# Wide norm factors: the row statistic by a ones-stationary matmul and one Newton step on a [128x256] tile in SBUF

## The chip, the core and the metric

The kernel runs on one core of one Trainium2 chip. The metric is the device time of one execution in microseconds (us), lower is better. A core has five engines that run their own instruction queues in order: TensorE (PE in the profile, with its weight loads as PEld), VectorE (DVE), ScalarE (ACT), GpSimd (POOL) and SyncE (SP, which only issues DMAs). They wait for each other on semaphores. PE writes into PSUM, here eight banks of [128x512] float32; the other data lie in SBUF.

## What is computed

A trunk of two layers on x of 512 tokens by 1024 channels, in float32. Layer 0 mixes tokens with stick-breaking attention, layer 1 with a diagonal state-space layer; each is followed by a gated MLP with a short causal convolution. Ahead of each of these four sub-layers, and once more at the end, stands an RMS norm, modulated by a conditioning vector:

```python
def rms_norm(x, g):
    y = x * lax.rsqrt(jnp.mean(x * x, axis=-1, keepdims=True) + EPS)
    return y * g

for i in range(DEPTH):                      # DEPTH = 2
    h = modulate(rms_norm(x, norm_mix[i]), sh1, sc1)
    x = x + g1 * (attention(h) if i == 0 else s5_ssm(h))
    h = modulate(rms_norm(x, norm_ffn[i]), sh2, sc2)
    x = x + g2 * conv_ffn(h)
return modulate(rms_norm(x, norm_out), sh, sc)
```

This case is about the factor rsqrt(mean(x*x) + EPS), one number per token, of which there are five sets of 512.

## The kernel before, in words

**Layout.** x lies in SBUF as eight tiles x[k] of [128 channels x 512 tokens] (`KD` = 8). The sum over channels is therefore a sum over the eight tiles and over the 128 partitions. Each product of the big matrices is made as three matmuls of a high and a low part (`mm3`, L169 to L175: L171 high by high, L174 high weights by low activations, L175 low weights by high activations), each 128x512, or 128x256 where only half of the tokens is done. `HALF` is the pair of token halves, columns 0 to 255 and 256 to 511.

**A joint.** Between two sub-layers the kernel does not wait for the norm of all tokens. `out_proj` (L360) makes the last product of a sub-layer: output tiles mt by mt, each added to x[mt] by `resid` (L350, DVE, L355), whose square (ACT, L244) is added to the running sum `acc` (DVE, L245). The last `TAIL` = 3 tiles (4 before the end of the program) are done for the first token half and then for the second (L404 to L416). While PE does the second half, the norm of the first half is worked out, and `head_mm` (L326) starts the next sub-layer's first four products with the first half, then does the second half, and the channels k = 6 and 7 for both. There are four joints: attention to MLP 0, MLP 0 to state-space layer, state-space layer to MLP 1, MLP 1 to output.

**The factor before.** For one half of a joint `rstd_stat` (L278) calls `rstd_y` (L258): for each 128 tokens a matmul with those columns of `acc` as stationary operand and a single column of ones as moving operand, which leaves the sums with tokens on partitions, a [128x2] tile in the PSUM bank `stat` (L266). ACT takes the square root (`nsd`, L270), DVE makes v (L271), the reciprocal (L272) and one Newton step of the inverse root (L273 to L275) on [128x2]. Two DVE instructions scale the unit matrix by it into `dg` (L283), a [128x256] tile of two diagonal blocks. Then `rstd_bc` (L286) multiplies ones with `dg` (L288): each of the 128 partitions of the PSUM bank `rbc` now holds the factor of each token along the free dimension, as `norm_tile` (L302) needs it for x * factor (DVE, L308). ACT then applies the modulation twice, to `hH` (L315) and to `nt` (L317), and DVE makes the low part `hL` (L321).

**What sets the order.** A scheduler orders each engine's queue, except for instructions that are pinned to their written order (`pe_pin`). The matmuls of the factor are pinned at a chosen place of PE's queue: the first half's `stat` ahead of product k = `STATK` = 0 of the second-but-last tile of the tail, and its `rbc` at `MIDK` or `MIDN` of the next tile; the second half's at `HEADS` = (1, 2) and `HEADB` = (3, 2) in the head, which are (k, product). So the factor's way through ACT and DVE is covered by matmuls that stand between.

**The two other uses.** At the program's start `rstd_y` is called for all 512 tokens (L605), and the start has `dg` and `rbc` of its own (L609 to L618). At the end, `last` (L1503) norms the first half as channels by tokens (`ft`, L1527 on DVE for k = 0, L1529 on POOL for the others, from an SBUF copy `bcs` of `rbc`, L1506; then ACT, L1531) and the second half as tokens by channels: `xa` (L1511, POOL) is transposed by PE, and the factor `y` of `rstd_y` (L1520, with `sq` of the last tile, L1508, as a second part) is a scalar per partition in L1543 (ACT, then POOL L1544) and L1546 (DVE). Eight stores follow (L1535, L1547).

Of the kernel before, what the change touches and what calls it, by code (L numbers as in the profile page):

```python
# [7 lines left out]
F32 = mybir.dt.float32  # L8
# [3 lines left out]
AF = mybir.ActivationFunctionType  # L12
ALU = mybir.AluOpType
# [3 lines left out]
P = 128  # L17
T = 512
D = 1024
# [9 lines left out]
NC = T // CH  # L29
EPS = 1e-6  # L30
NW = 5
MIDK = 1
STATK = 0
HEADK = 6
HEADS = (1, 2)
HEADB = (3, 2)
HEADW = (4, 8, 11, 13)
UPRE = 12
NACC = 6
# [20 lines left out]
NPRE = 3  # L60
KPRE = 5
NWT = 4
MIDN = 2
TAIL = 3
QK = 'kq'
BGA = 3
# [23 lines left out]
def _trunk(ctx, tc, I, out, tap):  # L90
# [10 lines left out]
    np_ = pool("np")  # L101
# [4 lines left out]
    def bank(p=None, name="ps"):  # L106
        p = p or mm
        return p.tile([P, 512], F32, tag="b", name=name)
# [14 lines left out]
    ident = consts[:, 0:128]  # L123
# [121 lines left out]
            V.tensor_tensor(acc[:, cr], acc[:, cr], sq[:, cr], ALU.add)  # L245

    def rstd_new(acc):
        return dict(acc=acc, ps=bank(aux, "stat"), dg=np_.tile([P, T], F32, tag="dg", bufs=1, name="dg"), bc={})

    def pe_pin(ins):  # L250
        tc.keep_in_program_order(ins)
# [1 line left out]
    def sqrt_table():  # L253

        warm = np_.tile([P, 64], F32, tag="warm", bufs=1, name="warm")[:, 0:1]
        tc.keep_in_program_order(S.activation(warm, ones[:, 0:1], AF.Sqrt))

    def rstd_y(R, cr, pinned=False, more=(), between=lambda: None):  # L258
        t0, t1 = cr.start // P, cr.stop // P
        ps = R["ps"]  # L260
        parts = [R["acc"]] + list(more)
        for q, part in enumerate(parts):
            if q:
                between()
            for i in range(t0, t1):
                ins = PE.matmul(ps[:, i:i + 1], part[:, i * P:(i + 1) * P], ones[:, 0:1], start=q == 0 and (i == t0 or len(parts) == 1), stop=q == len(parts) - 1 and (i == t1 - 1 or q == 0))  # L266
                if pinned:
                    pe_pin(ins)
        v, sd, y, t = (np_.tile([P, 4], F32, tag=g, bufs=2, name=g)[:, :t1 - t0] for g in ("nv", "nsd", "ny", "ntm"))
        R["nsd"] = S.activation(sd, ps[:, t0:t1], AF.Sqrt, bias=epst, scale=1.0 / D)  # L270
        V.tensor_scalar(v, ps[:, t0:t1], 1.0 / D, EPS, ALU.mult, ALU.add)  # L271
        V.reciprocal(y, sd)  # L272
        V.tensor_tensor(t, y, y, ALU.mult)  # L273
        V.scalar_tensor_tensor(t, v, -0.5, t, ALU.mult, ALU.mult)
        V.scalar_tensor_tensor(y, t, 1.5, y, ALU.add, ALU.mult)  # L275
        return y

    def rstd_stat(R, cr, pinned=False):  # L278
        t0, t1 = cr.start // P, cr.stop // P
        dg = R["dg"]  # L280
        y = rstd_y(R, cr, pinned)
        for i in range(t0, t1):
            ins = V.tensor_scalar(dg[:, i * P:(i + 1) * P], ident, y[:, i - t0:i - t0 + 1], None, ALU.mult)  # L283
        return ins

    def rstd_bc(R, cr, pl, pinned=False):  # L286
        bc = bank(pl, "rbc")
        ins = PE.matmul(bc[:, cr], ones, R["dg"][:, cr], start=True, stop=True)  # L288
        if pinned:
            pe_pin(ins)  # L290
        R["bc"][cr.start] = bc

    def new_h():
        hh = [hp_.tile([P, T], F32R, tag=f"hH{k}", name=f"hH{k}") for k in range(KD)]
# [31 lines left out]
    def head_mm(R, h, a, b, hd):  # L326
        pin["head"] = []
        todo = [(k, HALF[0]) for k in range(HEADK)] + [(k, HALF[1]) for k in range(HEADK)] + [(k, FULL) for k in range(HEADK, KD)]
        made = 0
        for n, (k, cr) in enumerate(todo):  # L330

            while made < (min(n + 3, HEADK) if cr == HALF[0] else n + 1):
                norm_tile(h, todo[made][0], R["bc"], a, b, todo[made][1])
                made += 1
            for q, (w, ps) in enumerate(hd):
                if cr == HALF[0] and (k, q) == HEADS:
                    rstd_stat(R, HALF[1], True)
                if cr == HALF[0] and (k, q) == HEADB:
                    rstd_bc(R, HALF[1], mm, True)
                mm3(ps[:, cr], wk(w, k), (h[0][k][:, cr], h[1][k][:, cr]), k == 0 and cr.start == 0, k == KD - 1)  # L340

    @contextmanager
# [17 lines left out]
    def out_proj(wsrc, rhs, gcol, acc2, nm, tail=TAIL, perm=False, n=D, after=lambda: None, part=(), last=None, head=None, getw=None, step=lambda: None, early={}):  # L360
# [46 lines left out]
        for q, (mt, w, ps) in enumerate(ws):  # L407
            mid = {}
            if q == 1:
                mid[STATK] = lambda: rstd_stat(R, ca, True)  # L410
            if q == 2:
                mid[MIDK if nk > 6 else MIDN] = lambda: rstd_bc(R, ca, aux, True)
            run(ps, w, cb, mid, pinned=True)
            if last and mt == KD - 1:
                resid(mt, ps, gate(mt), cb, None, perm)
                last(R)  # L416
            else:
                resid(mt, ps, gate(mt), cb, acc2, perm)
# [1069 lines left out]
    with ExitStack() as fctx:  # L1488
# [13 lines left out]

        def last(R):  # L1503
            op, a, brow = F_["op"], F_["a"], F_["brow"]
            bcs = op.tile([P, H], F32, tag="bcs", name="bcs")
            bci = S.activation(bcs, R["bc"][0][:, ca], AF.Copy)  # L1506
            sq = op.tile([P, T], F32, tag="sq", name="sq7")
            sqi = V.tensor_tensor(sq[:, cb], x[KD - 1][:, cb], x[KD - 1][:, cb], ALU.mult)  # L1508
            xa = [op.tile([P, H], F32, tag=f"xa{k}", name=f"xa{k}") for k in range(KD)]
# [13 lines left out]
            for q, k in enumerate(FORD):  # L1523
                t = op.tile([P, H], F32, tag="t", bufs=4, name="ft")
                with behind_head([sqi] if k else [bci]), behind_head([R["nsd"]]) if q >= FINA else ExitStack():
                    if k < FINV:
                        V.tensor_tensor(t, x[k][:, ca], R["bc"][0][:, ca], ALU.mult)  # L1527
                    else:
                        G.tensor_tensor(t, x[k][:, ca], bcs, ALU.mult)  # L1529
                    if q < FINS:  # L1530
# [108 lines left out]
```

## Time and profile before

| | |
|---|---|
| runs (3) | median 1175.27 us, 1175.04 to 1179.25 us |
| the profiled execution: span from the first to the last instruction | 1174.0 us (the profile gives no other time of its own for that execution) |
| granted TensorE clock, mean | 0.995 |
| PE busy | 1158.9 us, 99% of the span, 6242 matmul records |
| DVE, ACT, POOL busy | 857.7 us (73%), 563.5 us (48%), 270.8 us (23%) |
| DMA | 211.01 MB, mean 180 GB/s |

How to read it. Times are in us from the start of the span, unless marked ns. A row of the timeline gives start, duration, engine, line of the kernel, operation, output<-inputs with shapes, how many instructions are merged, and in brackets how long the engine was idle before it and what ended that. The chain of waits is followed back from the last instruction; its rows give start, duration, engine, tile and line. A float32 matmul (`stat`, `rbc`) leaves two records each. Matmul records overlap, so the cost of a matmul on PE is read from the starts of its neighbours or from the chain, not from its duration.

### The profile page before, as it was taken

What the parts mean: (1) busy time and instruction counts of PE and PEld (TensorE: products, weight loads), DVE (VectorE), ACT (ScalarE), POOL (GpSimd) and SP (SyncE); (2) the same over time, 40 slices, a digit from 0 to 9 for tenths busy, and PEclk for the clock granted to TensorE, in tenths of its full rate; (3) what the DMA queues carried; (4) which work ended last, traced back from release to release, by engine and by line L of the source; (5) the groups of instructions that cost most, each with busy time, mean ns of one, the idle gap of its engine ahead of it and who ended that gap; (6) DMA issues with size and microseconds to landing.
All of it is one profiled execution on the core that took longest, in us unless ns stands there. A gap on an engine that the chain in (4) does not pass through costs nothing.

```text
span 1174.0 us, 16592 instructions
## 1 busy us (share of the span) xinstructions
PE 1158.9 (99%) x6242; PEld 964.2 (82%) x6242; DVE 857.7 (73%) x1311; ACT 563.5 (48%) x896; POOL 270.8 (23%) x278
## 2 busy tenths in 40 slices
PE   8999999999999999999999999999999999999997
PEld 7887777699788888888889888789888888888887
DVE  6968888775998666787757599887598378744555
ACT  6756667456453244413346477647443144422443
POOL 2001110000298799979800000000000000000003
PEclk8999999999999999999999999999999999999999
DMA  8873656331267858797756598671176357432322
GB/s 320 292 264 116 192 162 195 111 123 55 78 189 268 247 167 252 198 292 253 230 151 223 149 353 293 207 255 50 49 231 217 107 153 184 133 123 73 92 69 72
DMA packets 91618, 211.01 MB, mean 180 GB/s; under 512 B 19601, under 2 KB 37905, under 8 KB 91538
## 3 DMA queue, kind: packets, MB, share of 16 engines
q1 hardware_dynamic: 78562, 191.08, 51.0%
q0 software_dynamic: 4656, 16.78, 4.5%
q10 hardware_dynamic: 8320, 2.10, 0.8%
q8 instruction: 49, 0.80, 0.3%
q14 instruction: 31, 0.25, 0.1%
HBM read 188.68 MB, written 21.24 MB: 179 GB/s over the span
## 4 chain that ended last, share of the span: by engine, by line
PE 78%; DVE 7%; issue 7%; DMA 5%; ACT 2%; POOL 1%; SPq 1%; POOLq 0%; DVEq 0%; ACTq 0%
PE up L171 13%; PE up L174 13%; PE up L175 13%; PE dn L171 6%; PE dn L174 6%; PE dn L175 6%; DMA wg<-in_w_modT_dram 3%; PE u L174 1%; PE u L171 1%; PE u L175 1%; PE wo L171 1%; PE wos L174 1%; PE wo L175 1%; PE wo L174 1%; PE wos L175 1%
## 5 line engine op out<-in xcount | busy, mean ns | idle before, releaser
L171 PE MATMUL up<-hH,up_h 128*128 128x512 f32 x640 | 249.7, 391 | 0.3 <-DVE ca L461 0.3
L175 PE MATMUL up<-hH,up_l 128*128 128x512 f32 x640 | 249.3, 390 | 0.3 <-DVE up_l L166 0.3
L174 PE MATMUL up<-hL,up_h 128*128 128x512 f32 x640 | 249.3, 390 | 0.0
L461 DVE SCALAR_TENSOR_TENSOR ca<-up,small,ca 128x511 f32<-128x511 f32 (+1 forms) x176 | 131.6, 748 | 120.7 <-ACT ca L459 117.6
L171 PE MATMUL dn<-gH,dn_h 128*128 128x512 f32 (+1 forms) x394 | 145.0, 369 | 0.0
L198 DVE SCALAR_TENSOR_TENSOR wg<-wg,cact 128x1024 f32<-128x1024 f32 x96 | 121.4, 1281 | 31.7 <-DMA wg<-in_w_modT_dram 31.6
L174 PE MATMUL dn<-gL,dn_h 128*128 128x512 f32 (+1 forms) x394 | 144.5, 367 | 0.0
L175 PE MATMUL dn<-gH,dn_l 128*128 128x512 f32 (+1 forms) x394 | 144.4, 366 | 0.0
L171 PEld LDWEIGHTS up<-hH,up_h 128*128 128x128 f32 x640 | 120.1, 188 | 26.5 <-issue 1.5
L175 PEld LDWEIGHTS up<-hH,up_l 128*128 128x128 f32 x640 | 120.1, 188 | 25.9 <-DVE up_l L166 1.1
L174 PEld LDWEIGHTS up<-hL,up_h 128*128 128x128 f32 x640 | 120.1, 188 | 24.4
L459 ACT ACTIVATE ca<-up,small 128x512 f32<-128x512 f32 x88 | 68.2, 775 | 149.5 <-PE up L175 149.5
L1511 POOL TENSOR_SCALAR xa<-x,Anorm_out 128x256 f32<-128x256 f32 x7 | 5.7, 818 | 570.3 <-DVE x L355 570.3
L165 ACT ACTIVATE up_h<-up_r 128x1024 fp32r<-128x1024 f32 x80 | 84.2, 1052 | 75.3 <-PE dn L174 58.1
L166 DVE TENSOR_TENSOR up_l<-up_r,up_h 128x1024 fp32r<-128x1024 f32 x80 | 116.3, 1454 | 5.4 <-ACT up_h L165 4.5
L355 DVE SCALAR_TENSOR_TENSOR x<-dn,mod,x 128x512 f32<-128x512 f32 (+1 forms) x55 | 37.4, 680 | 71.4 <-PE dn L175 71.4
L171 PEld LDWEIGHTS dn<-gH,dn_h 128*128 128x128 f32 x394 | 74.3, 189 | 12.9 <-issue 0.6
L174 PEld LDWEIGHTS dn<-gL,dn_h 128*128 128x128 f32 x394 | 74.3, 189 | 12.1
L175 PEld LDWEIGHTS dn<-gH,dn_l 128*128 128x128 f32 x394 | 74.3, 189 | 12.1
L165 ACT ACTIVATE dn_h<-dn_r 128x1024 fp32r<-128x1024 f32 (+1 forms) x48 | 46.7, 982 | 46.2 <-PE dn L174 38.5
L166 DVE TENSOR_TENSOR dn_l<-dn_r,dn_h 128x1024 fp32r<-128x1024 f32 (+1 forms) x48 | 61.6, 1283 | 0.8 <-ACT dn_h L165 0.5
L477 ACT ACTIVATE gH<-gm 128x512 fp32r<-128x512 f32 x44 | 27.1, 616 | 67.3 <-DVE gm L473 67.3
(349 smaller groups left out, 2311.0 us busy)
## 6 DMA issues: line engine op xcount, KB each, us to landing
up_r<-in_w_up_dram SPq DMA_DIRECT2D x80, 512.0 KB
wg<-in_w_modT_dram SPq DMA_DIRECT2D x71, 512.0 KB
dn_r<-in_w_down_dram SPq DMA_DIRECT2D x32, 512.0 KB
wg<-in_w_modT_dram POOLq DMA_DIRECT2D x25, 512.0 KB, 4.0
wgs<-in_w_modT_dram SPq DMA_DIRECT2D x16, 512.0 KB
dn_r<-in_w_down_dram SPq DMA_DIRECT2D x16, 384.0 KB
wv_r<-in_w_v_dram SPq DMA_DIRECT2D x8, 512.0 KB
wk_r<-in_w_qk_dram SPq DMA_DIRECT2D x8, 512.0 KB
```

The source lines that it names most:

```text
L165: order("S", lambda: S.activation(wh[:, :n], raw[:, :n], AF.Copy))
L166: pin["split"] = order("V", lambda: V.tensor_tensor(wl[:, :n], raw[:, :n], wh[:, :n].bitcast(F32), ALU.subtract))
L171: ins = PE.matmul(ps, ah, bh, start=start, stop=False)
L174: PE.matmul(ps, ah, bl, start=False, stop=False)
L175: PE.matmul(ps, al, bh, start=False, stop=stop)
L198: mul = lambda: V.scalar_tensor_tensor(w, w, 1.0, cact, ALU.mult, ALU.mult, accum_out=raw[:, col:col + 1])
L355: add = lambda: V.scalar_tensor_tensor(xs, pv, gate, xs, ALU.mult, ALU.add)
L459: follow("S", lambda: S.activation(ca, ps, AF.Identity, bias=small[:, cb:cb + 1], scale=tapw[2]))
L461: follow("V", lambda: V.scalar_tensor_tensor(ca[:, q:], ps[:, :T - q], tapw[2 - q], ca[:, q:], ALU.mult, ALU.add))
L477: follow("S", lambda: S.activation(gh, m, AF.Copy))
L1511: G.tensor_scalar(xa[k], x[k][:, cb], a[:, k:k + 1], 0.0, ALU.mult, ALU.add)
```

## The change

For the four joints, `rstd_stat` now multiplies with `ones` as the stationary operand and the 256 columns of `acc` as moving operand: `stat` holds the sums of squares [128x256], the same on every partition, which is the layout that `norm_tile` needs. ACT takes the inverse root by its table (`Abs_reciprocal_sqrt`) from PSUM straight into `dg`, now an SBUF tile that holds the factors themselves, and DVE does one Newton step on [128x256] with three instructions, through a temporary `ntw` that shares the two buffers of `sq`. The product with `dg` and the two banks of `rbc` at each joint go, and so does the copy `bcs` at the end; `norm_tile` and the last stage read `dg` from SBUF. For k = 6 and 7 of the head `norm_tile` now takes 512 columns at once. `rstd_y`, which remains at the start and for the last half, loses the reciprocal. The table that is loaded ahead of it is that of the new function; both programs have 11 table loads, at the same places.

```diff
-MIDK = 1
-HEADB = (3, 2)
-MIDN = 2
...
     def rstd_new(acc):
-        return dict(acc=acc, ps=bank(aux, "stat"), dg=np_.tile([P, T], F32, tag="dg", bufs=1, name="dg"), bc={})
+        dg = np_.tile([P, T], F32, tag="dg", bufs=1, name="dg")
+        return dict(acc=acc, ps=bank(aux, "stat"), dg=dg, bc=dg)
...
-        tc.keep_in_program_order(S.activation(warm, ones[:, 0:1], AF.Sqrt))
+        tc.keep_in_program_order(S.activation(warm, ones[:, 0:1], AF.Abs_reciprocal_sqrt))
...
-        v, sd, y, t = (np_.tile([P, 4], F32, tag=g, bufs=2, name=g)[:, :t1 - t0] for g in ("nv", "nsd", "ny", "ntm"))
-        R["nsd"] = S.activation(sd, ps[:, t0:t1], AF.Sqrt, bias=epst, scale=1.0 / D)
+        v, y, t = (np_.tile([P, 4], F32, tag=g, bufs=2, name=g)[:, :t1 - t0] for g in ("nv", "ny", "ntm"))
+        R["nsd"] = S.activation(y, ps[:, t0:t1], AF.Abs_reciprocal_sqrt, bias=epst, scale=1.0 / D)
         V.tensor_scalar(v, ps[:, t0:t1], 1.0 / D, EPS, ALU.mult, ALU.add)
-        V.reciprocal(y, sd)
...
     def rstd_stat(R, cr, pinned=False):
-        t0, t1 = cr.start // P, cr.stop // P
-        dg = R["dg"]
-        y = rstd_y(R, cr, pinned)
-        for i in range(t0, t1):
-            ins = V.tensor_scalar(dg[:, i * P:(i + 1) * P], ident, y[:, i - t0:i - t0 + 1], None, ALU.mult)
-        return ins
-
-    def rstd_bc(R, cr, pl, pinned=False):
-        bc = bank(pl, "rbc")
-        ins = PE.matmul(bc[:, cr], ones, R["dg"][:, cr], start=True, stop=True)
+        ps, y = R["ps"][:, cr], R["dg"][:, cr]
+        ins = PE.matmul(ps, ones, R["acc"][:, cr], start=True, stop=True)
         if pinned:
             pe_pin(ins)
-        R["bc"][cr.start] = bc
+        t = np_.tile([P, T], F32, tag="sq", bufs=2, name="ntw")[:, :cr.stop - cr.start]
+        S.activation(y, ps, AF.Abs_reciprocal_sqrt, bias=epst, scale=1.0 / D)
+        V.scalar_tensor_tensor(t, y, -0.5 / D, y, ALU.mult, ALU.mult)
+        V.scalar_tensor_tensor(t, ps, D * EPS, t, ALU.add, ALU.mult)
+        R["y"] = V.scalar_tensor_tensor(y, t, 1.5, y, ALU.add, ALU.mult)
...
-                if cr == HALF[0] and (k, q) == HEADB:
-                    rstd_bc(R, HALF[1], mm, True)
...
-            if q == 2:
-                mid[MIDK if nk > 6 else MIDN] = lambda: rstd_bc(R, ca, aux, True)
...
-            bcs = op.tile([P, H], F32, tag="bcs", name="bcs")
-            bci = S.activation(bcs, R["bc"][0][:, ca], AF.Copy)
+            bcs, bci = R["bc"][:, ca], R["y"]
...
                     if k < FINV:
-                        V.tensor_tensor(t, x[k][:, ca], R["bc"][0][:, ca], ALU.mult)
+                        V.tensor_tensor(t, x[k][:, ca], bcs, ALU.mult)
                     else:
                         G.tensor_tensor(t, x[k][:, ca], bcs, ALU.mult)
```

**What stands where.** The line numbers of the changed kernel are some lines lower for the same code. First, PE in the first joint, head of MLP 0, where the second half's statistic stands (`up` are the four head products, `upo` their weights, `hH` and `hL` the high and low parts of one channel tile each; the number tells which). Before:

```order
L171 MATMUL up_1_1_2603<-hH_2582,upo_h 128x256
L266 MATMUL stat<-ones,acc 128x1 x2
L174 MATMUL up_0_0_2600<-hL_2590,upo_h 128x256
L175 MATMUL up_0_0_2600<-hH_2582,upo_l 128x256
L174 MATMUL up_0_1_2601<-hL_2590,upo_h 128x256
```

Now:

```order
L168 MATMUL up_1_1_2591<-hH_2571,upo_h 128x256
L277 MATMUL stat<-acc,ones 128x256
L171 MATMUL up_0_0_2588<-hL_2579,upo_h 128x256
L172 MATMUL up_0_0_2588<-hH_2571,upo_l 128x256
L171 MATMUL up_0_1_2589<-hL_2579,upo_h 128x256
```

Two narrow matmuls behind the first four products of channel tile k = 2 (hH_2582 is the third of its set, hH_2580 the first) have become one wide one behind those of k = 3 (hH_2571, with hH_2568 the first), one group of twelve matmuls further down the queue.

Second, DVE at the same place (`up_2_0_l` is the low part of a later weight tile, `nt` the product x * factor; nt_2728 and nt_2706 are those of k = 0 for the second half). Before:

```order
L271 TENSOR_SCALAR nv<-stat 128x2
L272 RECIPROCAL ny<-nsd 128x2
L273 TENSOR_TENSOR ntm<-ny 128x2
L321 TENSOR_TENSOR hL_2592<-nt_2667,hH_2584 128x256
L274 SCALAR_TENSOR_TENSOR ntm<-nv,ntm 128x2
L275 SCALAR_TENSOR_TENSOR ny<-ntm,ny 128x2
L283 TENSOR_SCALAR dg<-consts,ny 128x128 x2
L166 TENSOR_TENSOR up_2_0_l<-up_2_0_r,up_2_0_h 128x1024
L321 TENSOR_TENSOR hL_2593<-nt_2685,hH_2585 128x256
L308 TENSOR_TENSOR nt_2728<-x_78,rbc 128x256
```

Now:

```order
L163 TENSOR_TENSOR up_2_0_l<-up_2_0_r,up_2_0_h 128x1024
L314 TENSOR_TENSOR hL_2581<-nt_2665,hH_2573 128x256
L282 SCALAR_TENSOR_TENSOR ntw<-dg 128x256
L283 SCALAR_TENSOR_TENSOR ntw<-stat,ntw 128x256
L284 SCALAR_TENSOR_TENSOR dg<-ntw,dg 128x256
L301 TENSOR_TENSOR nt_2706<-x_78,dg 128x256
```

The factor stood ahead of the split of `up_2_0` and its product `nt` behind it; now the factor's three instructions stand behind the split, with `nt` right after them.

Third, POOL in the last stage. Before:

```order
L1511 TENSOR_SCALAR xa_10713<-x_83,Anorm_out_9925 128x256
L1529 TENSOR_TENSOR ft<-x_79,bcs 128x256
L1529 TENSOR_TENSOR ft<-x_80,bcs 128x256
L1529 TENSOR_TENSOR ft<-x_81,bcs 128x256
L1529 TENSOR_TENSOR ft<-x_82,bcs 128x256
L1511 TENSOR_SCALAR xa_10714<-x_84,Anorm_out_9925 128x256
```

Now:

```order
L1517 TENSOR_TENSOR ft<-x_79,dg 128x256
L1517 TENSOR_TENSOR ft<-x_80,dg 128x256
L1517 TENSOR_TENSOR ft<-x_81,dg 128x256
L1499 TENSOR_SCALAR xa_10633<-x_83,Anorm_out_9857 128x256
L1517 TENSOR_TENSOR ft<-x_82,dg 128x256
L1517 TENSOR_TENSOR ft<-x_83,dg 128x256
```

Three of the products with the factor moved ahead of an `xa`, which waits for the residual of a later tile.

## The prediction

> **What bounds the kernel now.** I read the page first, then the chain of waits, PE's own waits, and the timelines at the four joints and in the last stage.
>
> ```profile
> span 1174.0 us, 16592 instructions
> PE 1158.9 (99%) x6242; PEld 964.2 (82%) x6242; DVE 857.7 (73%) x1311; ACT 563.5 (48%) x896; POOL 270.8 (23%) x278
> PE 78%; DVE 7%; issue 7%; DMA 5%; ACT 2%; POOL 1%; SPq 1%; POOLq 0%; DVEq 0%; ACTq 0%
> ```
>
> PE is occupied for 99% of the span and makes up 78% of the chain. So a matmul that goes shortens the span, as long as PE doesn't then wait for something that hasn't moved. Whether it waits now is told by PE's waits from 600 to 700 us, the one stretch with a joint in which it does:
>
> ```profile
> PE stat L266 <- DVE acc L245: 0.3, 1, 0.3
> PE u L174 <- DVE hL L321: 0.2, 1, 0.2
> ```
>
> Both belong to joint 2, and neither is the factor: `stat` waits there for the running sum, and `hL` of k = 0 stands behind the residual of the last tile, which waits for PE itself. Around the factor PE runs from matmul to matmul in every joint.
>
> **The change part by part.** *PE's matmuls.* The chain in the fourth joint shows what the two old products cost, by the pitch of their neighbours:
>
> ```profile
> 1157.30 0.12 PE dn L175
> 1157.42 0.34 PE stat L266 x4
> 1157.76 0.22 PE dn L171
> 1157.98 0.12 PE dn L174
> ...
> 1160.74 0.45 PE rbc L288 x2
> L288 PE MATMUL rbc<-dg,ones x14: 376/377/380, 259.6 to 1160.8; 128*128 128x256 f32 x14
> ```
>
> A plain 128x256 product takes 0.12. The statistic takes 0.34 and lengthens its successor by 0.10: 0.44. `rbc` takes 0.45. The new statistic has the form of `rbc` (ones by 128x256, float32, two records), so I price it at 0.45. A half-joint thus loses 0.44 + 0.45 and gets 0.45: 0.44 less. The 14 records of `rbc` are seven half-joints (two in each of three joints, one at the end): 7 x 0.44 = 3.1 us. Bounds per half: 0.34 if the new product delays its successor by 0.10 on top of its 0.45, and 0.51 if it costs no more than one of its records (0.38): 2.4 to 3.6 us.
>
> *The factor's way through ACT and DVE.* It is off PE's path if it is done before PE needs the first `hH` of that half. The tightest place is the second half in a head, here in joint 1:
>
> ```profile
> 265.94 0.50 PE L266 MATMUL stat<-ones,acc 128*128 128x1 f32 x4
> 266.48 0.26 ACT L270 ACTIVATE nsd<-stat,epst 128x2 f32<-128x2 f32 x1 [0.64 <-PE stat L266]
> 266.77 0.16 DVE L271 TENSOR_SCALAR nv<-stat 128x2 f32<-128x2 f32 x1 [0.64 <-ACT nsd L270]
> 267.13 1.04 ACT L165 ACTIVATE up_h<-up_r 128x1024 fp32r<-128x1024 f32 x1
> 267.33 0.64 PE L171 MATMUL up<-hH,upo_h 128*128 128x256 f32 x4
> 267.81 0.28 PE L174 MATMUL up<-hL,upo_h 128*128 128x256 f32 x1
> 267.98 0.48 DVE L283 TENSOR_SCALAR dg<-consts,ny 128x128 f32<-128x128 f32 x2
> 268.38 1.22 DVE L166 TENSOR_TENSOR up_l<-up_r,up_h 128x1024 fp32r<-128x1024 f32 x1
> 270.81 0.75 DVE L308 TENSOR_TENSOR nt<-x,rbc 128x256 f32<-128x256 f32 x2 [0.87 <-PE rbc L288]
> 271.26 0.60 ACT L315 ACTIVATE hH<-nt,mod,Anorm_ffn 128x256 fp32r<-128x256 f32 x1 [2.10 <-DVE nt L308]
> 272.02 0.63 PE L171 MATMUL up<-hH,upo_h 128*128 128x256 f32 x4
> ```
>
> Before, the way from `stat` (265.94) to `hH` (271.86) took 5.9 us, most of it a wait for the place of `rbc` in PE's queue, and was ready 0.16 ahead of PE. The new way has no second visit to PE. Its pieces come from these rows:
>
> ```profile
> 279.68 0.80 ACT L315 ACTIVATE hH<-nt,mod,Anorm_ffn 128x512 fp32r<-128x512 f32 x1
> 1161.20 0.38 ACT L1506 ACTIVATE bcs<-rbc 128x256 f32<-128x256 f32 x1 [0.15 <-PE rbc L288]
> L321 DVE TENSOR_TENSOR hL<-nt,hH 128x256 fp32r<-128x256 f32 x36 | 15.3, 424 | 7.8 <-ACT nt L317 7.6
> L355 DVE SCALAR_TENSOR_TENSOR x<-dn,mod,x 128x256 f32<-128x256 f32 x14 | 6.8, 482 | 5.2 <-PE dn L175 5.2
> ```
>
> The inverse root on [128x256] isn't in the trace. Its bounds are a plain copy out of PSUM (0.38) and an activation with two operands per partition (0.60). I take 0.47: `nsd`'s 0.26, plus 0.20 for 256 more columns (0.80 less 0.60). The three wide DVE instructions lie between 0.42 (two SBUF inputs, `hL`) and 0.48 (one from PSUM, the residual): 0.42 + 0.48 + 0.42 = 1.32. From the start of `stat`: 0.54 to ACT, 0.47, 0.03 to DVE, 1.32, `nt` 0.41 (as now), 0.04, `hH` 0.60: 3.4 us. `stat` now stands one group later. The group's start was 267.33 and its `hL` products 267.81; less 0.44 (the old pair above it) and 0.44 (the half before), it starts at 266.93, so `hH` is ready at 270.3. PE comes for it at 272.02 less 0.88 = 271.14. That is 0.8 us in hand instead of 0.16. So I cost this way at nothing, and what hides it are the 24 products between. Without the cover each 0.1 beyond 0.8 costs PE 0.1 in that head. What stands behind the new waits: on ACT one square of the residual's sum (0.2 later in the first half), on DVE one addition to `acc`. Neither is waited for by PE before the next `stat`. A first half gets the same shortening, with the tail's last products between it and the head.
>
> DVE's sum per half hardly changes: five small instructions (about 0.9 with their gaps) and 0.48 for `dg` against 1.32. The 512-wide `nt`, the copy `bcs` and the two banks free time on engines that don't bound.
>
> *The last stage.* The chain there runs from the last residual over `sq`, the root and y to the last tiles:
>
> ```profile
> 1161.67 3.03 POOL L1529 TENSOR_TENSOR ft<-x,bcs 128x256 f32<-128x256 f32 x4 [0.56 <-ACT bcs L1506]
> 1163.67 0.43 DVE L245 TENSOR_TENSOR acc<-acc,sq 128x256 f32<-128x256 f32 x1 [0.54 <-ACT sq L244]
> 1165.13 2.29 POOL L1529 TENSOR_TENSOR ft<-x,bcs 128x256 f32<-128x256 f32 x3
> 1165.32 0.83 DVE L1508 TENSOR_TENSOR sq<-x 128x256 f32<-128x256 f32 x1
> 1167.22 0.15 DVE L272 RECIPROCAL ny<-nsd 128x2 f32<-128x2 f32 x1
> 1167.40 0.16 DVE L273 TENSOR_TENSOR ntm<-ny 128x2 f32<-128x2 f32 x1
> 1168.05 0.69 ACT L1543 ACTIVATE fn<-fin,ny 128x512 f32<-128x512 f32 x1
> 1168.82 1.27 POOL L1544 TENSOR_TENSOR fn<-fn,brow 128x512 f32<-128x512 f32 x1 [1.40 <-ACT fn L1543]
> ```
>
> Without the reciprocal the next instruction starts 0.18 earlier (1167.40 less 1167.22), and everything behind y with it: 0.2. POOL's seven `ft` start as soon as the factor is there, some 1.7 us earlier than 1161.67 (by the pieces above from `stat` at 1157.26: 0.54 + 0.47 + 0.03 + 1.32, plus one 0.43 addition that stands between, 1160.05), which takes them off the end of the chain, where y remains. I count nothing more for that.
>
> *The start.* The same reciprocal goes from the chain to the first product:
>
> ```profile
> 17.47 0.17 DVE L272 RECIPROCAL ny<-nsd 128x4 f32<-128x4 f32 x1
> 17.68 0.16 DVE L273 TENSOR_TENSOR ntm<-ny 128x4 f32<-128x4 f32 x1
> 18.33 1.63 POOL L613 TENSOR_SCALAR dg<-consts,ny 128x128 f32<-128x128 f32 x2 [3.86 <-DVE ny L275]
> ```
>
> 0.2 at most, nothing if the first weights then bound; I take 0.1.
>
> *The sum:* 3.1 + 0.2 + 0.1 = 3.4 us. Span 1174.0 less 3.4 is 1170.6. The median of the runs, 1175.27, lies 1.3 above the profiled span, so the forecast is **1171.9 us**, 0.3% less. A measurement of this kernel can tell about 0.5%, 5.9 us, from no change, so this counts as the same.
>
> **The rivals.** *A, the gain is partly used up.* The state-space layer and the end of MLP 0 have places where PE meets DVE and DMA chains. Those start from PE's own products and should move along; for it speaks that PE's waits there are short, against it that some loads could be bound to the clock rather than to PE. If the 1.3 us of joints 1 and 2's first three halves are lost, 1173.2.
>
> *B, a shared port.* `nt`, `ft` and the Newton step now read two SBUF tiles on DVE, where before one came from PSUM. In the last stage POOL reads SBUF at the same time. DVE's `sq` there took 0.83, against 0.43 for the same shape in `acc`; yet that `acc` also ran beside POOL's `ft`, and the `ft` kept 0.76 each throughout (3.03 by 4, 2.29 by 3). If each overlap costs 0.40 and POOL is the one held, by four DVE instructions, its `ft` end 1.6 later, close to where they end now; ACT takes `fn` behind the last `ft`, so the 0.2 of y and the last half-joint's 0.44 are lost: 1172.5. The other joints have no POOL work to collide with:
>
> ```profile
> 255.00:290.00 35.00, 35.00 (x254) 32.85 (x253) 20.09 (x54) 20.49 (x37) 0.18 (x2) 1.00 0.16 46
> 618.00:653.00 35.00, 34.42 (x273) 33.42 (x272) 26.48 (x64) 24.47 (x44) 0.00 (x0) 1.00 0.52 183
> ```
>
> (The fifth figure with a count is POOL's.) By the Trainium skill ("SBUF — State Buffer", "Who interferes with whom") a DVE instruction with two SBUF inputs contends with a GpSimd instruction that reads SBUF, and one with at most one SBUF input does not; that rule speaks against this change, and this rival is what it would do here. The trace agrees for `sq` (0.83) and doesn't for `acc` (0.43).
>
> *C, the factor comes late in the heads (slower than before).* In the two MLP heads the factor now stands on DVE behind the split `up_l` (1.22), whose ACT half `up_h` (1.04) stands ahead of the new root. The first half's work comes about 1.7 us earlier than before (as POOL's `ft` above) and the old root, for which ACT sat idle 0.64, is gone from ahead of `up_h`: from 267.13 that is 264.8, and the split is done by 267.1, 0.8 before the root (266.93 + 0.54 + 0.47 = 267.9). If none of the 1.7 comes through, it is 0.9 late, which uses up what is in hand. At worst all 2.3 us of the split stand before the factor; and if the three wide instructions took 0.83 each like `sq`, 1.2 more. Less the 0.8 in hand, PE would wait 2.7 in each of these two heads and 0.4 in the third: 5.8 lost for 3.4 gained, 1177.7. It decides from a way 1.7 us longer than my 3.4 + 0.8 in two heads. Against it: PE doesn't wait at all there now, with the split in the same queue.
>
> *D, more than the matmuls.* The statistic's weights were the data just summed, now they are ones that can be loaded ahead; the last stores may also come out of a queue that POOL's earlier `ft` relieve. If joints save 0.3 more per half and the end 1.0: another 3.1, 1168.8.
>
> **How the numbers follow.** The forecast has 0.60, A 0.12, B 0.08, C 0.08, D 0.12. The range must leave out no more than 0.2: it takes the forecast, A and B with their bounds, and reaches up to no change and down to D: 1168.8 to 1175.2. Faster by over 0.5% means below 1169.4: D, 0.12. Slower by over 0.5% means above 1181.1: the far part of C, 0.05. Within 0.5%: 0.83.
>
> **What the profile of the changed kernel would show.** Seven `stat` products 128x256 with about 0.45 in the chain and no `rbc` at the joints; PE without new waits in the heads; the root about 0.47, the Newton instructions 0.42 to 0.48; the first `hH` of a head's second half ready well before PE; POOL's first `ft` near 1.7 us earlier against the last half's `stat`. I'm wrong if PE waits for `hH` or `nt` in a head, if the root takes over 0.7, if a table load joins, or if the distance between the joints grows by what the joints lose.

## The result, and the profile after

| | before | after |
|---|---|---|
| median of 21 runs each | 1176.49 us (1173.87 to 1183.01) | 1179.95 us (1176.31 to 1184.49) |
| ratio, 95% interval | | 1.0029 (1.0019 to 1.0039) |
| span of the profiled execution | 1174.0 us | 1182.0 us |

The change makes the kernel slower by 0.3%, 3.4 us; the forecast was 3.4 us less. The profiled execution is one of the longer ones (1183.82 us), so its 8.0 us over the profile of before are not the size of the effect. Single executions of either kernel spread over 8 to 9 us, so times are compared below by medians and intervals. One of the eleven executions of the second experiment below took 2978 us and is left out of its ratio.

The page of after says that PE was not relieved, although it has 28 records fewer. The columns are as before:

```profile
span 1182.0 us, 16501 instructions
PE 1164.3 (99%) x6214; PEld 961.0 (81%) x6214; DVE 858.2 (73%) x1275; ACT 564.5 (48%) x895; POOL 270.8 (23%) x278
PE 84%; DMA 6%; DVE 5%; ACT 2%; issue 1%; POOL 1%; SPq 0%; POOLq 0%; ACTq 0%; DVEq 0%
```

PE's busy time has grown by 5.4 us, with fewer instructions. Some 3.4 of these belong to this one execution (see "The changed kernel again"); a second profile of the same kernel has 1161.0 us, 2.1 more than before. Before looking for a new wait, one should therefore ask whether the remaining instructions have become longer. First the parts that the forecast spoke of. The new instructions, grouped by line (duration in ns: least, median, most):

```profile
L281 ACT ACTIVATE dg<-stat,epst x7: 459/475/476, 255.9 to 1166.5; 128x256 f32<-128x256 f32 x7
L282 DVE SCALAR_TENSOR_TENSOR ntw<-dg x7: 421/425/426, 256.4 to 1167.0; 128x256 f32<-128x256 f32 x7
L283 DVE SCALAR_TENSOR_TENSOR ntw<-stat,ntw x7: 419/419/424, 257.1 to 1167.7; 128x256 f32<-128x256 f32 x7
L284 DVE SCALAR_TENSOR_TENSOR dg<-ntw,dg x7: 417/425/426, 257.6 to 1168.1; 128x256 f32<-128x256 f32 x7
```

The root takes 0.475 us (forecast 0.47) and the three Newton instructions 1.27 (1.32). The second half of the first head, from the timeline of after:

```profile
266.13 0.59 PE L277 MATMUL stat<-acc,ones 128*128 128x256 f32 x2
266.38 0.47 PE L171 MATMUL up<-hL,upo_h 128*128 128x256 f32 x1
266.68 0.28 PE L172 MATMUL up<-hH,upo_l 128*128 128x256 f32 x1
266.80 0.28 PE L171 MATMUL up<-hL,upo_h 128*128 128x256 f32 x1
...
266.76 0.47 ACT L281 ACTIVATE dg<-stat,epst 128x256 f32<-128x256 f32 x1 [0.42 <-PE stat L277]
267.27 0.42 DVE L282 SCALAR_TENSOR_TENSOR ntw<-dg 128x256 f32<-128x256 f32 x1 [0.32 <-ACT dg L281]
...
269.11 0.60 ACT L308 ACTIVATE hH<-nt,mod,Anorm_ffn 128x256 fp32r<-128x256 f32 x1 [1.87 <-DVE nt L301]
270.38 0.65 PE L168 MATMUL up<-hH,upo_h 128*128 128x256 f32 x4
```

The wide statistic holds PE for 0.25 and its successor for 0.30 instead of 0.12: 0.43, forecast 0.45. From `stat` to the end of the first `hH` it is 3.58 us (269.71 less 266.13; forecast 3.4), and PE comes for it at 270.38, 0.67 later (forecast 0.8). So the head does not wait for the factor, and the mechanism of the forecast stands. What has grown lies elsewhere. The count of `dn` matmuls in the same 30 us of MLP 0, in which PE runs without a pause (columns: stretch, length, busy time of PE with its count, granted clock, DMA share, GB/s), before and then after:

```profile
360.00:390.00 30.00, 30.00 (x134) 1.00 0.72 242
```

```profile
360.00:390.00 30.00, 30.00 (x130) 1.00 0.75 251
```

The same matmuls, untouched by the diff, without a pause and at full clock: 134 before and 130 now. From the starts of successive records, a 512-column matmul of `dn` steps 226.7 ns before and 233.3 ns after; `wos` likewise; `up`, `v` and `k` keep 227 in the median. A `dn` matmul of 256 columns steps 120 ns before. After, 135 of 248 such steps are 113 or 114 ns and most others 117 to 119, 115.4 in the mean.

What tells `dn` and `wos` from `up` is where their moving operand lies. The addresses that the two programs give to their buffers, modulo 256 bytes:

| buffer | before | after |
|---|---|---|
| moving operand of `up`, `k`, `q`, `glu` (hH, hL) | 64 | 64 |
| moving operand of `dn` (gH, gL) and `wos` (gzH, gzL) | 64 | **0** |
| stationary operand, the split weights (wH, wL) | 64 | 64 |

The change no longer needs the square root's small tile `nsd`, [128x4] in two buffers, which took 64 bytes of each partition. With it gone, the buffers of the sub-layers that are allocated behind it, gH and gzH among them, moved down by 64 bytes. Some PSUM banks changed too: in MLP 0 banks 2 and 3 have changed places, so that the third bank of the tiled up-projection is now 2 instead of 3.

### The profile page after: what moved, and what is told of

Same layout as the page of the kernel before. It is cut to its first block, busy times and chain, and to the rows that moved or that the text cites. A ratio compares the mean times of both kernels' runs of the same rounds, so it can differ in the third digit from the quotient of the medians.

```text
span 1182.0 us, 16501 instructions
## 1 busy us (share of the span) xinstructions
PE 1164.3 (99%) x6214; PEld 961.0 (81%) x6214; DVE 858.2 (73%) x1275; ACT 564.5 (48%) x895; POOL 270.8 (23%) x278
## 4 chain that ended last, share of the span: by engine, by line
PE 84%; DMA 6%; DVE 5%; ACT 2%; issue 1%; POOL 1%; SPq 0%; POOLq 0%; ACTq 0%; DVEq 0%
PE up L168 13%; PE up L172 13%; PE up L171 13%; PE dn L168 6%; PE dn L171 6%; PE dn L172 6%; PE o L815 2%; PE t L799 2%; DMA wg<-in_w_modT_dram 1%; PE wos L171 1%; PE k L168 1%; PE q L172 1%; PE q L168 1%; PE k L172 1%; PE k L171 1%; PE q L171 1%
## 5 line engine op out<-in xcount | busy, mean ns | idle before, releaser
L171 PEld LDWEIGHTS dn<-gL,dn_h 128*128 128x128 f32 x394 | 73.9, 188 | 14.2
```

The source lines that it names most:

```text
L171: PE.matmul(ps, ah, bl, start=False, stop=False)
```

## The experiments

The theories A, A', A'', B and C of this section explain the loss. They are not the rivals A to D of the prediction.

**Putting the addresses back.** The tile is reserved again and used by nothing; the order of the instructions on every engine stays that of the changed kernel, and so do its PSUM banks.

```diff
-        v, y, t = (np_.tile([P, 4], F32, tag=g, bufs=2, name=g)[:, :t1 - t0] for g in ("nv", "ny", "ntm"))
+        v, _, y, t = (np_.tile([P, 4], F32, tag=g, bufs=2, name=g)[:, :t1 - t0] for g in ("nv", "nsd", "ny", "ntm"))
```

> The changed kernel, but the small tile nsd (two buffers of 32 bytes a partition) stays reserved though nothing uses it, so that every buffer behind it stands at the SBUF address that it has before the change; the order of the instructions on each engine is that of the changed kernel. Theory A (addresses): in the changed kernel the buffers gH, gL, gzH and gzL stand 64 bytes lower, and a matmul of 512 columns that reads them takes 233.3 ns from start to start instead of 226.7, one of 256 columns 113.3 instead of 120. A expects 226.7 and 120 here, and 930 + 120 matmuls of 512 columns by 6.67 ns (7.0 us) less 252 of 256 columns by 6.67 (1.7) = 5.3 us less than the changed kernel: 1174.6, ratio to before 0.998. Theory B (the rotation of the PSUM banks, which the change moves too: the up-projection's third bank is 2 instead of 3): 233.3 ns as in the changed kernel, 1180. Theory C (waits at the head of the state-space layer's output projection, followed by 6.8 us at half clock): the step of dn stays whatever the address, 1180, or 1176.5 if the half clock stays away.

Measured: 1174.32 us (12 runs), before 1175.74 on the same chip, ratio 0.9983 (0.9968 to 0.9997). The same window of its trace:

```profile
360.00:390.00 30.00, 30.00 (x134) 1.00 0.74 236
```

134 again, 226.7 and 120 ns a step. One tile that nothing reads turns a kernel slower by 0.29% into one faster by 0.17%. Theory B falls, since all matmuls write the PSUM banks of the changed kernel.

**Moving the addresses of the kernel before.** The opposite edit: one more unused tile beside `nsd`, so that gH and its like go from 64 to 128 modulo 256.

```diff
-        v, sd, y, t = (np_.tile([P, 4], F32, tag=g, bufs=2, name=g)[:, :t1 - t0] for g in ("nv", "nsd", "ny", "ntm"))
+        v, sd, _, y, t = (np_.tile([P, 4], F32, tag=g, bufs=2, name=g)[:, :t1 - t0] for g in ("nv", "nsd", "npad", "ny", "ntm"))
```

> The kernel before, with one more small tile (two buffers of 32 bytes) that nothing uses beside nsd, so that every buffer behind it stands 64 bytes higher: the same parity in units of 64 bytes as in the changed kernel. Nothing else differs. Theory A (addresses): dn and wos of 512 columns 233.3 ns, of 256 columns 113.3: 5.3 us more than before, 1181.8, ratio 1.0045. Theories B (PSUM banks) and C (waits and half clock): 226.7 ns, ratio 1.000.

Measured: 1178.28 us, ratio 1.0018 (1.0006 to 1.0031). So moving addresses alone makes the kernel before slower. The size was missed, and the window shows why:

```profile
360.00:390.00 30.00, 30.00 (x133) 1.00 0.74 246
```

The steps now cycle through 226, 229 and 232 ns, 229 in the mean, and 256 columns take about 118. Thus 64 bytes up is not the same as 64 bytes down, and my parity in units of 64 bytes was too simple. With 2.2 ns by 1,050 matmuls less 2 ns by 252 one gets 1.8 us, ratio 1.0015.

**The step by address, measured by itself.** The first probe walks the moving operand's start past a stationary operand that stands still, then the other way round. `PROBE` holds 16 offsets in float32 elements, from 0 to 112.

```diff
...
+    for n in (512, 256, 384, 128):
+        for o in PROBE:
+            for q in range(20):
+                pe_pin(PE.matmul(ps[:, :n], pa[1][:, 512:640], pa[0][:, o:o + n], start=True, stop=True))
+    for o in PROBE:
+        for q in range(20):
+            pe_pin(PE.matmul(ps, pa[1][:, 512 + o:640 + o], pa[0][:, 16:528], start=True, stop=True))
```

> The changed kernel with 1,600 matmuls behind its last work, whose results nobody uses: 20 in a row for each of 16 start addresses (0 to 448 bytes past a buffer that starts 64 bytes past a multiple of 128) of the moving operand, with 512, 256, 384 and 128 columns, and then for 16 start addresses of the stationary one with 512 columns. Only the steps from start to start are read, not the time. Theory A (addresses): with 512 columns 226.7 ns at 0 bytes, 128, 256 and 384 past it, 233.3 at 64, 192 and 320 past it; with 256 columns 120 and 113.3 the other way round; offsets between these show how fine the rule is; the stationary operand's address changes nothing. Theory B (PSUM banks): one step for all addresses.

Measured with 512 columns, mean step in ns over the last 15 of each 20, by the moving start modulo 256: 226.7 and 226.9 at 64 (0 and 256 bytes past), 228.9 twice at 128, 233.1 and 232.1 at 192, 233.3 and 233.5 at 0. So the period is 256 bytes, not 128. Smaller offsets help no more: 8 bytes past the good place costs 233.3, 16 bytes 231.5, 32 bytes 233.4. The second half contradicts the last sentence of theory A: with the moving start at 128, the stationary start at 64, 128, 192 and 0 gives 228.9, 226.9, 233.5 and 232.3. So for starts that are multiples of 64 bytes it is the distance between the two that counts. Between these places the distance alone does not tell: 16 bytes cost 231.5 with the moving operand at 80 and the stationary at 64, but 228.5 at 128 and 112, and with the stationary operand 16 bytes ahead of the moving one (128 and 144) the step is the good 226.7. 384 columns step 173.2 to 176.7 with no rule to be seen, and 128 columns 111.5 to 111.9, whatever the address.

A second probe takes all 16 pairs:

```diff
...
+    for n in (512, 256):
+        for s in range(4):
+            for m in range(4):
+                for q in range(24):
+                    pe_pin(PE.matmul(ps[:, :n], pa[1][:, 496 + 16 * s:624 + 16 * s], pa[0][:, 48 + 16 * m:48 + 16 * m + n], start=True, stop=True))
```

> The changed kernel with 768 matmuls behind its last work, whose results nobody uses: 24 in a row for each pair of start addresses modulo 256 bytes, the stationary operand at 0, 64, 128 and 192, the moving one at 0, 64, 128 and 192, with 512 and with 256 columns. Only the steps are read. Theory A' (distance moving minus stationary modulo 256): with 512 columns 226.7 ns at distance 0, 228.9 at 64, 232 to 233 at 128, 233.4 at 192, whatever the addresses themselves; with 256 columns 120, 118, 118 and 113.3. Theory A'' (the moving address alone): the step depends on the moving operand's place and is the same for all four places of the stationary one.

Measured, mean step in ns over the last 18 of each 24, the four values of a row being the four places of the stationary operand (0, 64, 128, 192):

| moving less stationary, modulo 256 | 512 columns | 256 columns |
|---|---|---|
| 0 | 227.2, 226.7, 228.1, 226.7 | 119.9, 119.7, 119.7, 119.7 |
| 64 | 228.9, 228.9, 228.9, 228.9 | 117.8, 117.8, 117.8, 117.8 |
| 128 | 232.5, 232.5, 233.3, 232.7 | 118.9, 118.9, 118.6, 118.5 |
| 192 | 233.3, 233.3, 233.3, 233.3 | 117.8, 117.8, 113.3, 113.3 |

For 512 columns A' holds in every row and A'' in none. For 256 columns at distance 192 there are two values, and the same pair of addresses (stationary 64, moving 0) stepped 113.3 in the first probe, both kinds in the changed kernel, and 117.8 here. What decides between the two stays open.

**Using the rule for the 256-column matmuls.** Half-tile products should gain where the 512-column ones lose, so the weights of the tails were shifted by 64 bytes inside their buffers (the tails have only 768 of 1024 columns, so there is room). The edit is on top of the first one; `off` is 16 for the tails alone.

```diff
...
+        wh, wl = wh[:, off:off + n], wl[:, off:off + n]
...
```

> The changed kernel with the small tile kept (as in e1), and in addition the weights of the last down-projection groups' tails stand 64 bytes further inside their buffers, so that the 252 matmuls of 256 columns read moving data that starts 64 bytes below the stationary data in units of 256 bytes. Order of the instructions as in the changed kernel. Theory A' (the step of a matmul depends on the distance of the two operands' addresses modulo 256 bytes): those 252 matmuls step 113.3 ns instead of 120, the 512-column ones stay at 226.7: 1.7 us less than e1, 1172.6, ratio to before 0.997. Theory A'' (the step depends on the moving operand's own address alone): no change from e1, 120 ns, 1174.3.

Measured: 1173.03 us, ratio 0.9974 (0.9958 to 0.9990): the fastest version, below the kernel before and the changed one. But the 252 steps went from 120 to 116.9 in the mean: 48 of them to 113 or 114, most others to 117 to 119. That is 0.8 us, not 1.7, so A' does not hold here as it stands. By its time the version is not told apart from the first experiment.

**One part of the change alone.** Only the table of the inverse root in the narrow factor, with the reciprocal gone:

```diff
-        R["nsd"] = S.activation(sd, ps[:, t0:t1], AF.Sqrt, bias=epst, scale=1.0 / D)
+        R["nsd"] = S.activation(y, ps[:, t0:t1], AF.Abs_reciprocal_sqrt, bias=epst, scale=1.0 / D)
...
-        V.reciprocal(y, sd)
```

> The kernel before with one part of the change alone: ScalarE's inverse-root function in the narrow factor, without the reciprocal; the narrow statistics, the product with dg and ones and all its banks stay, and all buffers stay where they are. By the prediction's steps this part is worth 0.2 us at the end and 0.1 at the start: 1175.4, ratio 0.9997; the other 3.1 us belong to TensorE's instructions. A theory that ScalarE's and VectorE's shorter chain is what pays expects most of e1's 2.0 us here: 1174.

Measured: 1175.94 us, ratio 0.9994 (0.9982 to 1.0007): no difference that can be told, as forecast. Its 0.3 us are below what 12 runs resolve, and the interval reaches to 2.1 us faster, so the time alone does not rule out the theory of the shorter chain. The traces speak against it: PE in the first experiment gains 1.07, 0.89, 1.41 and 0.64 us at the four joints on this run too, as much as on the kernel before (below), so the gain belongs to what this run lacks.

**Doubling the new statistic.** On top of the first experiment:

```diff
-        ins = PE.matmul(ps, ones, R["acc"][:, cr], start=True, stop=True)
+        for q in range(2):
+            ins = PE.matmul(ps, ones, R["acc"][:, cr], start=True, stop=True)
...
```

> e1 (the changed kernel at the old addresses) with each of the seven wide statistics matmuls issued twice into the same place, the second one overwriting the first with the same sums. If TensorE's time at the joints is on the path in full, as the prediction's first step has it, 7 x 0.45 = 3.1 us more than e1: 1177.4, ratio 1.0015. If TensorE only waits less where it works more (the rival that the gain is used up), half of it or less: 1175.9 or below.

Measured: 1175.39 us, ratio 0.9989 (0.9978 to 1.0000), 0.7 us more than the first experiment by the ratios. The intervals of the two are too wide to settle it, so the traces are compared by the starts of the same matmuls. PE falls behind the first experiment's trace by 0.41 to 0.57 at each of the seven places, 3.2 in sum. It regains 0.4 at the start of the state-space layer's `wos`, where it otherwise waits for gzH, and 0.2 over the products of `u`. So the price per matmul was right, and both theories have a part: some of the time saved ahead of `wos` is spent waiting there.

**The changed kernel again.** Unchanged code, because the first profile of after had a stretch that the others had not:

> The changed kernel itself once more, for a second profile and on the chip of e6. The address theory expects 233.3 ns a step in dn and wos again and 5.3 us more than e1: 1179.6, ratio to before 1.003. The theory of the extra stretch at half clock (6.8 us at half speed after the waits at the head of the state-space layer's output projection, worth 3.4 us) expects that stretch again at that place; the address theory expects no such stretch to belong to the change, so that it may be absent or stand elsewhere.

Measured: 1178.86 us, ratio 1.0025 (1.0010 to 1.0041), with 233.3 ns a step. PE in the three stretches around that place in the first profile:

```profile
757.00:763.00 6.00, 4.61 (x19) 1.00 0.29 95
763.50:770.00 6.50, 5.63 (x14) 0.50 0.74 230
771.00:777.00 6.00, 6.00 (x28) 1.00 0.54 175
```

and in the second:

```profile
757.00:763.00 6.00, 5.14 (x22) 1.00 0.34 126
763.50:770.00 6.50, 6.50 (x29) 1.00 0.61 185
```

At a granted clock of 0.50, 14 matmuls instead of 29: about 3.4 us lost in that execution. The second profile has none of it, at the same place and with the same slow `dn`. So theory C falls as a cause of the difference. The stretch explains part of the 8.0 us between the two profiled spans. Matched matmul by matmul, this second profile falls behind the first experiment's by 6.0 us in `dn` and 0.75 in `wos` with 512 columns, and gains 1.2 in `dn` and 0.3 in `wo` with 256: 5.25 us in sum. The two spans differ by 5.4 (1176.7 and 1171.3).

**A larger dose.** If addresses are the cause, moving hH and hL must cost far more, as `up` has more matmuls than `dn`. The kernel before, with padding ahead and compensation behind:

```diff
+    hp_.tile([P, 48], F32, tag="hpad", name="hpad")
     np_ = pool("np")
+    np_.tile([P, 16], F32, tag="npad", name="npad")
```

> The kernel before with 192 bytes of padding ahead of the buffers hH and hL (also oH and oL) and 64 bytes behind them, both unused, so that these buffers alone change their place modulo 256 bytes; the order of the instructions stays. Theory A' (distance of the operands modulo 256 bytes): 2,724 matmuls of 512 columns (up 1,920, q and k 384, wo 120, u 108, glu 192) go from distance 0 to 192 and from 226.7 to 233.3 ns a step, 18.2 us, and 192 of v to distance 64, 0.4 us; those of 256 columns may give back up to 2 us: 1193 to 1195, ratio 1.014 to 1.016. Theory A'' (the moving buffer's own place alone, as with gH at 768): the same for these, nothing for v. If addresses did not matter: 1176.

Measured: 1188.9 us (4 runs), ratio 1.0107 (1.0088 to 1.0126), 12.6 us more. The window of `up`, before and then here:

```profile
420.00:480.00 60.00, 58.49 (x256) 1.00 0.74 230
```

```profile
420.00:480.00 60.00, 58.49 (x249) 1.00 0.72 223
```

`up`, `k`, `q`, `wo`, `u` and `glu` step 233 ns, `v` 228.9, and `dn`, which did not move, keeps 226.7: the steps are as A' has them, that of `v` too, and A'' falls again. The sum was too high by 4 to 6 us. Part of it is that `q`, `k`, `u`, `wo` and `glu` step 228 to 230 on average before, not 226.7, and that 144 matmuls of 256 columns in `wo` gave back 5 ns each in the mean. Matched matmul by matmul, all that moved is 14.2 us slower instead of 18.6. In the profiled execution PE's waits at six places are also 2.5 us shorter in sum, which leaves about 12, against 12.6 measured.

## Why the prediction was wrong

**The step that failed is the sum.** It reads 3.1 + 0.2 + 0.1, with terms for the instructions that the diff adds, removes and moves. The instructions that it leaves alone were put at nothing, without a reason: a `dn` matmul was taken to cost what it cost before. But the diff also removes a tile, so that 1,050 matmuls of 512 columns changed their distance to the weights from 0 to 192. In the second profile of the changed kernel they took 6.4 ns more each in the mean (6.74 us) than in the first experiment's, while 252 of `dn` and 144 of `wo` with 256 columns took 4.6 and 2.3 less (1.49 us): 5.25 us slower. (The expectation of the first experiment reaches 5.3 from 7.0 less 1.7; both terms were somewhat too large.) Measured, as the ratios of the changed kernel less that of the first experiment: 0.0046 and 0.0042, 5.4 and 4.9 us. No rival had it; C, the one that ended slower, puts the loss into waits in the heads, and these didn't come.

**PE's matmuls: right, at the upper end.** 0.43 for the wide statistic against 0.45. The lead of the first experiment over the profile of before, by the same matmuls, grows by 1.04 over joint 1, 0.89 over joint 2, 1.18 over joint 3 and 0.65 over joint 4 with the last stage: 3.8 us against 3.1 + 0.2. Less the 0.2 of the last stage that is 0.51 per half, the upper bound that the working gave. For joint 3, before:

```profile
760.70 0.39 PE L175 MATMUL wos<-gzH,wos_l 128*128 128x512 f32 x1
...
830.02 0.40 PE L174 MATMUL up<-hL,up_h 128*128 128x512 f32 x1
```

and in the first experiment:

```profile
759.89 0.39 PE L172 MATMUL wos<-gzH,wos_l 128*128 128x512 f32 x1
...
828.03 0.40 PE L171 MATMUL up<-hL,up_h 128*128 128x512 f32 x1
```

0.81 ahead at its start, 1.99 at its end.

**The factor's way: right.** 3.58 us against 3.4, 0.67 in hand against 0.8, no wait for `hH` in either MLP head. Rival C is refuted for the factor.

**Rival A: right in kind.** Two places take back what the joints gave. In the state-space layer, before:

```profile
759.08 0.39 PE L175 MATMUL wos<-gzH,wos_l 128*128 128x512 f32 x1
759.31 0.39 PE L171 MATMUL wos<-gzH,wos_h 128*128 128x512 f32 x1
760.36 0.50 PE L174 MATMUL wos<-gzL,wos_h 128*128 128x512 f32 x1 [0.67 <-DVE gzL L1438]
```

and in the first experiment:

```profile
757.35 0.39 PE L172 MATMUL wos<-gzH,wos_l 128*128 128x512 f32 x1
758.18 0.49 PE L168 MATMUL wos<-gzH,wos_h 128*128 128x512 f32 x1 [0.45 <-ACT gzH L1426]
759.56 0.50 PE L171 MATMUL wos<-gzL,wos_h 128*128 128x512 f32 x1 [0.88 <-DVE gzL L1427]
```

PE comes 1.73 earlier and leaves 0.80 earlier, as gzH and gzL do not come as much sooner: 0.9 given back. At 321 us in MLP 0 it is the split `up_l` on DVE, before and then in the first experiment:

```profile
320.58 0.39 PE L174 MATMUL up<-hL,up_h 128*128 128x512 f32 x1
320.92 0.50 PE L175 MATMUL up<-hH,up_l 128*128 128x512 f32 x1
```

```profile
320.70 0.39 PE L171 MATMUL up<-hL,up_h 128*128 128x512 f32 x1
321.47 0.50 PE L172 MATMUL up<-hH,up_l 128*128 128x512 f32 x1 [0.38 <-DVE up_l L163]
```

From 0.12 to 0.55 behind: 0.43 given back. (That execution came 1.2 us late out of the attention; this varies between the profiles of the changed kernel.) This wait for `up_l` is 0.3 to 0.4 long in all profiles with the wide factor and at most 0.13 in the four with the narrow one, so it belongs to the change. The 0.9 is less firm: the traces of the shifted tails and of the doubled statistic give back 0.5 there. Together 1.3 us, or 1.36 unrounded. A had named the state-space layer, as it was, and the end of MLP 0, where the place found is near its start. That A's sum was 1.3 too is luck, since it was three half-joints' worth of matmuls.

**A term that nobody had.** PE's waits from 600 to 700 us in the profile of before have a third row, the longest, which the prediction does not show:

```profile
PE pv L1280 <- issue: 1.3, 1, 1.3
```

The same view of the first experiment has no such row:

```profile
PE u L171 <- DVE hL L314: 0.4, 1, 0.4
PE stat L277 <- DVE acc L242: 0.3, 1, 0.3
```

The row of before is PE's wait, up to 668.50, ahead of the first `pv` of the state-space layer. That `pv` starts 1.69 us behind the last `u` matmul in the kernel before, and 0.32 behind it in the first experiment. The four profiles with the narrow factor have 0.8 to 1.8 of such a wait, the seven with the wide one 0 to 0.33. The lead of the first experiment grows by 1.40 at this place, a gain beyond the matmuls. That is rival D's kind of gain; at the two places that D names, the joints and the last stores, little or nothing of it is seen. Why the wait goes is open.

Added up, from the end of the attention to the end of the program, the lead of the first experiment's trace grows by 3.76 at the joints, less 1.36, plus 1.40: 3.8 us. The median of its runs is 2.0 us faster (0.4 to 3.8). The trace thus lies at the edge of the interval, and how much of the 1.36 and the 1.40 an average execution has is not settled. The forecast of 3.4 lies between the two numbers, but that does not confirm its sum, which has neither term. With the measured 2.0 faster and the 5.25 of the layout, the changed kernel should be about 3.3 slower; it is 3.4 (2.2 to 4.6).

**The last stage: right, and rival B half right.** From after:

```profile
1165.87 0.59 PE L277 MATMUL stat<-acc,ones 128*128 128x256 f32 x2
...
1168.65 2.50 POOL L1517 TENSOR_TENSOR ft<-x,dg 128x256 f32<-128x256 f32 x3 [1.52 <-DVE dg L284]
1168.97 0.70 DVE L1515 TENSOR_TENSOR ft<-x,dg 128x256 f32<-128x256 f32 x1
...
1169.60 0.95 DVE L242 TENSOR_TENSOR acc<-acc,sq 128x256 f32<-128x256 f32 x1
```

POOL's `ft` start 2.78 us behind the last half-joint's first statistic, where it was 4.41 before: 1.6 earlier, as forecast. DVE's `ft`, now with two SBUF inputs beside POOL, takes 0.70, where it took 0.42 beside POOL with one input from PSUM, and an `acc` there takes 0.95. By the Trainium skill ("SBUF — State Buffer", "Who interferes with whom") a DVE instruction with two SBUF inputs contends with a GpSimd instruction that reads SBUF; the trace agrees, and more clearly than the profile of before. Both engines are held. POOL's seven `ft` take 0.72 to 0.74 each but for three of 0.91 to 0.92; before, there were two such, 0.93 beside the `acc` of 0.43 and 0.91 beside `sq`. The prediction's "0.76 each throughout" is a mean that hid them, and beside that `acc` POOL was the one that took longer. DVE now loses up to 0.5 in one instruction, and POOL has one more long `ft`, 0.2, where B had 1.6 of delay. PE does not wait for either, and the lead over before grows by 0.65 up to the end, so no cost of it is seen.

## What to carry to other kernels

A diff changes the memory layout as well as the instructions: list the SBUF address of each operand of the most frequent instruction in both programs before summing terms. When a busy engine gets busier with fewer instructions, first compare the pace of untouched instructions in a stretch without waits, before looking for new waits. If a small edit fails by a fraction of a per cent, put the old layout back by an unused tile and time that, since the edit itself may have been good.

## What the runs showed of the hardware that was not expected

The pace of a stream of float32r matmuls with 128x128 weights depends on where the moving and the stationary operand start in SBUF. For starts at multiples of 64 bytes it goes by their distance modulo 256 bytes: with 512 columns 226.7 to 228.1 ns at 0, 228.9 at 64, 232.1 to 233.3 at 128, 233.3 to 233.5 at 192. With 256 columns it is the other way round, 119.7 at distance 0 and 113.3 or 117.8 at 192. Between multiples of 64 the distance alone does not fix the step (228.5 and 231.5 at 16 bytes).

The Trainium skill ("SBUF — State Buffer", "Who interferes with whom") gives TensorE two read ports, one for the moving operand and one for the weight load, and calls them independent. Nothing in that leads one to expect a pace that hangs on the distance of the two; here it does, by 6.6 ns in 227. Where the two reads meet, if they do, no run here shows.

A stretch of 6.8 us at a granted clock of 0.50 came in the middle of one profiled execution of the changed kernel and not in another, so a single profile can be 3.4 us off for that reason alone. Another such stretch begins at 12 to 14 us in seven of the nine profiles without probes, 10.2 us long in one of these, and is missing in two.
